# Head norms and merge sums in tiles of their own, the values' split apart from their transfer, sigmoids after the last exponentials, and the norm of x in pieces

## The chip, the cores and the metric

The kernel runs on one core of one Trainium2 chip. The metric is the device time of one execution in microseconds (us). Of the kernel before there are three timed runs and one profiled execution; all times below are of these.

## What is computed

One layer of a hybrid decoder trunk on 1024 positions of width 1024, in float32. Cut to what matters here:

```
h   = rms_norm(x, pre_mix_g)
qa, ka, va, qb, kb, vb, gates = split(h @ w_in)
# A: 4 heads, two maps of 64 columns each, values of 128
p   = softmax(causal(rope(qa) rope(ka)^T * scale))      # two maps for each head
oa  = (p[0] - lam * p[1]) @ va
oa  = rms_norm(oa, diff_head_g) * (1 - lam_init)        # the head norm
ya  = oa @ w_a_out
# B: 3 dilated groups (dilations 1, 4, 16), 4 heads of 128 each
o_g, lse_g = dilated_group(qb[g], kb[g], vb[g])         # softmax in a window
wts = softmax(stack(lse_g))                             # over the groups
yb  = sum(wts[g] * o_g) @ w_b_out                       # the merge
g_a, g_b = split(sigmoid(gates))
x   = x + rms_norm((g_a * ya + g_b * yb) @ w_mix_out, post_mix_g)
x   = x + rms_norm(conv_glu(rms_norm(x, pre_ffn_g)), post_ffn_g)
```

## The kernel before

A float32 operand is kept as two parts, a high one (`whi`, `xh`, `kh`, `vh`, `oah`), which ScalarE (ACT) copies out, and the low rest, which VectorE (DVE) subtracts (`split`, L149 and L146; `wlo`, `xl`, `kl`, ...). A product is then three matmuls on TensorE (PE): high by high, low by high, high by low (`mm3`, L154 to L156). `raw` is a weight as loaded.

The stages follow one another. **Values** (to about 160 us): the columns of V for all heads, by a scheme with seven products `p1` to `p7` for two halves `i` and four slices `k`, 56 steps `n`, that reads x unscaled. The evacuations go to `yv` (L471) and are stored to `v_d` by POOL's queue. Beside this run, at fixed steps, the angles, the norm of x (`norm_x`, sixteen squares, L389), the sines (L394), and `make_tables`: it spreads the norm's factor `rstd` over a row, transposes it on TensorE into a PSUM tile `acc`, and multiplies the tables of sine and cosine with it there (L406 to L408). `acc` is also what the products go to.

**Heads** (A, about 200 to 530 us): for each of four heads, eight blocks of queries. Scores (L717, L718) go to `s`, DVE adds the mask and takes the maximum (L720), ACT takes exponentials (L729), DVE joins both maps (L735), TensorE transposes them (L649, into `pt`), ACT and DVE split the transposed tile, and TensorE multiplies it with the values (`pv`, L662 and L665), into `o` and then `osb` (L759). After four blocks comes `head_norm`: the square `sq` of `osb` (L786), sums by products with ones (L794), a reciprocal root, the copy `spread` (L797), its transposes (L802). `sq` and `spread` come from the pool `rt` under the tags `t1` and `t2`, two buffers each, that the rotated projections (copies out of PSUM at L636, L637 to L639) and the gates (L249) also use. `jobs` yields after each block and runs what `later(n, fn)` has put on its clock of blocks; `interleave` puts pieces of the projections of the next head and of the gates, and values, between, as the letters of `A_FILLS` say.

**Groups** (B, about 530 to 915 us): twelve steps, one for a pair of heads, a group and a head, each with four blocks, the same way: mask and maximum (L921), exponentials (L928), the result `osb` to `og_d`. Values of a pair and group come back from `v_d` by `fetch_values` (SP's queue, tile `vperm`) and are split by ACT and DVE; `proj_b` makes q, then k of the next step (`kh`, L832). `merge(h)` joins the three groups of a head: from the sums' rows come weights, stored to `e_d`, loaded again broadcast as `mw` (L1019), beside the results `og` (L1021), both on POOL's queue; then `og` times `mw` in place (L1027), two sums into `og` itself (L1028, L1029), and a split or a store from there, for one half of the positions and then the other.

**Outputs** (from about 915 us): `branch` loads gates (`gl`), takes their sigmoid (L1092), and multiplies the merged results with the output weights; then the mix and the feed-forward part.

A tile framework orders the instructions of each engine: it simulates engine times, `high_priority` moves work ahead, and a tile with `bufs` buffers makes its next user wait for the readers of the last. Each engine then runs its list strictly in order.

Of the kernel before, what the change touches and what calls it, by code (L numbers as in the profile page):

```python
# [24 lines left out]
P = 128  # L25
# [24 lines left out]
START_GATES, A_FILLS, B_GATES = 1, ("gpgg", "gpvgg", "wgpgg", "gPVgg"), 3  # L50
SLOTS = 18
LEFT_PAD = 32


XT_BUFS, ANGLES_AT, NORM_AT, SINES_AT, TABLES_AT, STORE_AT = 6, 15, 18, 22, 29, {26: 0, 28: 3, 31: 2, 34: 1}
# [32 lines left out]
def trunk(ctx: ExitStack, tc: tile.TileContext, a, out):  # L88
# [119 lines left out]
    dma(gpre, a["pre_mix_g"])  # L208
# [174 lines left out]
    def norm_x():  # L383

        ssx = tiny.tile([P, 2, 32], F32, name="ssx", bufs=1)[:, :, :8]
        for m in range(8):
            for half, sl in enumerate(halves()):
                t = load_raw(a["x"][m * P : (m + 1) * P, sl], next(tags))
                nc.scalar.activation(t, t, AF.Square, accum_out=ssx[:, half, m : m + 1])  # L389
        tt(ssx[:, 0], ssx[:, 0], ssx[:, 1], ALU.add)  # L390
        nc.vector.tensor_copy(rstd, rsqrt(ssx[:, 0], D, tb, "rx"))
# [5 lines left out]
    def make_tables(*tab):  # L397
# [3 lines left out]
        for half, sl in enumerate(halves()):  # L401
            row = psum()
# [3 lines left out]
            nc.vector.scalar_tensor_tensor(neg[:, sl], tab[0][:, sl], -1.0, row, op0=ALU.mult, op1=ALU.mult)  # L406
            nc.vector.tensor_tensor(tab[0][:, sl], tab[0][:, sl], row, op=ALU.mult)
            nc.vector.tensor_tensor(tab[1][:, sl], tab[1][:, sl], row, op=ALU.mult)  # L408
# [18 lines left out]
    with ExitStack() as st_y:  # L427
# [12 lines left out]
        def fetch_v(n):  # L440
# [3 lines left out]
            got_v[n] = [load_raw(a["w_v"][j * 4 + k][:, (2 * i + c) * 512 : (2 * i + c + 1) * 512], next(tags), parts=1 if n else 2)  # L444
                        for c, j in which]

        def ready_v(n, w=512):
# [12 lines left out]
            for c in range(0, 512, w):  # L460
                split(*(t[:, c : c + w] for t in ready[n]), src[:, c : c + w])
# [67 lines left out]
        with ExitStack() as st0:  # L529
# [14 lines left out]
            for _ in range(4):  # L544
                nc.tensor.matmul(idle[:, :256], zeros[:, :P], zeros[:, :256], start=True, stop=True)
            for j in range(KC):
# [5 lines left out]
                for c in range(0, 512, w):  # L552
                    split_x(K_FIRST[j], slice(c, c + w), xts[j][:, c : c + w])
                    if c == 0:
                        ready_v(j, w)
# [18 lines left out]
        for n in range(8, len(steps_v)):  # L574
# [7 lines left out]
            if n == NORM_AT:  # L582
                norm_x()
# [115 lines left out]
    def attend_a(h, i, ops, vs, out_sb, pair):  # L699
# [52 lines left out]
        def add(b):  # L752
# [908 lines left out]
```

## Time and profile before

| | us |
|---|---|
| median of 3 runs (1754.65, 1761.11, 1761.55) | 1761.11 |
| profiled execution | 1758.33 |
| its span | 1756.6 |
| busy: PE / DVE / ACT / POOL | 1704.4 / 1345.0 / 893.7 / 100.6 |

The mean granted TensorE clock was 0.989 of full speed. The page cuts the span in 40 slices of 43.9 us and gives the busy share of each in tenths, 9 for 90% or more:

```profile
PE   9989998999989999989999999999999999999997
DVE  8884686777675676767656766699999999789977
ACT  7634564546343676546763633364444444355453
PEclk9999999999989999999999999999999999999999
DMA  8685311131212222532276442023222222196624
```

Slice 13 (about 483 to 527 us) has the clock at 0.8; the values fill the first four, the heads slices 6 to 12, the groups 13 to 21.

### The profile page before, as it was taken

Reading aid. Unit: us, or ns where it says so; the run is one execution under the profiler, and the core shown is the slowest. Engines: PE = TensorE matmul, PEld = TensorE weight load, DVE = VectorE, ACT = ScalarE, POOL = GpSimd, SP = SyncE. Lnnn points to the kernel's source line nnn. Section 1 sums busy time; section 2 is a strip of 40 time slices with the busy share of each in tenths; the row PEclk is TensorE's granted clock in tenths of the full one; section 3 lists DMA queues with packets and bytes.
Section 4 is the critical chain, followed back from the end, with each engine's and each line's share of the span. In section 5 each row is a group of like instructions: output and inputs, shape, how many; then the busy total and the mean of one; then the engine's idle time right before and its main releaser. Section 6 shows DMA issues by size and latency. Waiting matters only on the chain.

```text
span 1756.6 us, 23087 instructions
## 1 busy us (share of the span) xinstructions
PE 1704.4 (97%) x8076; PEld 1419.9 (81%) x8076; DVE 1345.0 (77%) x2558; ACT 893.7 (51%) x1648; POOL 100.6 (6%) x163
## 2 busy tenths in 40 slices
PE   9989998999989999989999999999999999999997
PEld 7778887788878888778878888878888888878886
DVE  8884686777675676767656766699999999789977
ACT  7634564546343676546763633364444444355453
POOL 0021000000000000200022410300000000000000
PEclk9999999999989999999999999999999999999999
DMA  8685311131212222532276442023222222196624
GB/s 254 195 303 183 111 61 39 40 102 59 80 61 77 74 73 74 176 114 73 82 257 233 160 156 96 36 73 108 90 78 97 78 78 96 55 336 217 215 84 156
DMA packets 105604, 216.42 MB, mean 123 GB/s; under 512 B 13120, under 2 KB 22272, under 8 KB 105488
## 3 DMA queue, kind: packets, MB, share of 16 engines
q1 hardware_dynamic: 91888, 176.79, 30.6%
q0 software_dynamic: 8704, 29.51, 5.0%
q10 hardware_dynamic: 4896, 8.65, 1.3%
q8 instruction: 63, 1.03, 0.2%
q14 instruction: 53, 0.43, 0.1%
HBM read 167.05 MB, written 47.86 MB: 122 GB/s over the span
## 4 chain that ended last, share of the span: by engine, by line
PE 49%; DVE 5%; DMA 4%; issue 2%; ACT 1%; POOL 0%; DVEq 0%; ACTq 0%; POOLq 0%; SPq 0%
PE acc L155 11%; PE acc L156 11%; PE acc L154 11%; PE acc L1497 3%; PE acc L1496 3%; PE acc L1495 3%; PE acc L1177 2%; PE acc L1179 2%; PE acc L1178 2%; PE pt L1495 1%; PE pt L1497 1%; PE pt L1496 1%; DMA og<-og_d 1%; DMA ot<-oa_d 1%; DVE t L1293 1%
## 5 line engine op out<-in xcount | busy, mean ns | idle before, releaser
L154 PE MATMUL acc<-xh,whi 128*128 128x512 f32 x768 | 306.8, 399 | 2.6 <-DVE gate L249 2.6
L155 PE MATMUL acc<-xh,wlo 128*128 128x512 f32 x768 | 306.4, 399 | 0.0
L156 PE MATMUL acc<-xl,whi 128*128 128x512 f32 x768 | 306.4, 399 | 0.0
L149 ACT ACTIVATE whi<-raw 128x512 fp32r<-128x512 f32 (+1 forms) x252 | 155.7, 626 | 218.9 <-PE acc L156 138.0
L146 DVE TENSOR_TENSOR wlo<-raw,whi 128x512 fp32r<-128x512 f32 (+1 forms) x252 | 177.2, 710 | 51.8 <-ACT whi L149 49.2
L154 PEld LDWEIGHTS acc<-xh,whi 128*128 128x128 f32 x768 | 146.4, 191 | 30.7 <-DVE gate L249 2.7
L155 PEld LDWEIGHTS acc<-xh,wlo 128*128 128x128 f32 x768 | 146.4, 191 | 28.2
L156 PEld LDWEIGHTS acc<-xl,whi 128*128 128x128 f32 x768 | 146.2, 190 | 28.0
L154 PE MATMUL acc<-mh,whi 128*128 128x512 f32 x400 | 155.8, 390 | 0.3 <-ACT mh L149 0.3
L155 PE MATMUL acc<-mh,wlo 128*128 128x512 f32 x400 | 155.6, 389 | 0.0
L156 PE MATMUL acc<-ml,whi 128*128 128x512 f32 x400 | 155.3, 389 | 0.0
L636 ACT ACTIVATE t<-acc 64x512 f32<-64x512 f32 (+1 forms) x160 | 94.7, 592 | 48.8 <-PE acc L156 42.7
L1373 DVE TENSOR_TENSOR u<-acc,u 128x512 f32<-128x512 f32 x133 | 90.6, 685 | 24.4 <-PE acc L156 24.3
L149 ACT ACTIVATE whi<-s 128x512 fp32r<-128x512 f32 x76 | 47.0, 628 | 108.3 <-PE acc L156 96.1
L637 DVE TENSOR_TENSOR t<-acc,cos 128x512 f32<-128x512 f32 x64 | 44.1, 689 | 58.5 <-ACT t L636 57.3
L154 PEld LDWEIGHTS acc<-mh,whi 128*128 128x128 f32 x400 | 75.1, 188 | 16.4 <-ACT mh L149 0.5
L155 PEld LDWEIGHTS acc<-mh,wlo 128*128 128x128 f32 x400 | 75.1, 188 | 15.6
L156 PEld LDWEIGHTS acc<-ml,whi 128*128 128x128 f32 x400 | 75.1, 188 | 15.6
L662 PE MATMUL o<-pt,vh 128*128 128x256 f32 (+1 forms) x376 | 72.3, 284 | 9.4 <-ACT pt L149 7.9
L1496 PE MATMUL acc<-whi,wlo 128*128 128x512 f32 x220 | 77.6, 390 | 0.0
L1495 PE MATMUL acc<-whi 128*128 128x512 f32 x220 | 76.5, 390 | 0.0
L662 PEld LDWEIGHTS o<-pt,vh 128*128 128x128 f32 x376 | 61.5, 197 | 16.0 <-ACT pt L149 8.9
(382 smaller groups left out, 3952.1 us busy)
## 6 DMA issues: line engine op xcount, KB each, us to landing
raw<-in_w_in SPq DMA_DIRECT2D x96, 256.0 KB, 2.9
raw<-in_w_up SPq DMA_DIRECT2D x88, 256.0 KB, 2.8
raw<-in_w_v SPq DMA_DIRECT2D x71, 256.0 KB, 4.0
raw<-c_d SPq DMA_DIRECT2D x48, 256.0 KB, 3.9
c_d<-c SPq DMA_DIRECT2D x22, 512.0 KB, 3.1
raw<-in_w_down SPq DMA_DIRECT2D x37, 256.0 KB, 3.6
v_d<-yv POOLq DMA_DIRECT2D x32, 256.0 KB, 5.3
gt_d<-gate ACTq DMA_DIRECT2D x32, 256.0 KB, 2.3
```

The costliest lines, as they stand in the source:

```text
L146: eng.tensor_tensor(lo, src, hi.bitcast(F32), op=ALU.subtract)
L149: nc.scalar.activation(hi, src, AF.Copy)
L154: nc.tensor.matmul(o, sh, mh, start=first, stop=False, skip_group_check=on)
L155: nc.tensor.matmul(o, sl, mh, start=False, stop=False, skip_group_check=on)
L156: nc.tensor.matmul(o, sh, ml, start=False, stop=last, skip_group_check=on)
L636: nc.scalar.activation(t1[dst], ps[src], AF.Copy)
L637: nc.vector.tensor_tensor(t2, ps, cos[:, sl], op=ALU.mult)
L662: nc.tensor.matmul(o[:, q0 : q1 + 1], vs[b // 4][0][:, b % 4, c], t[:, part], start=first and n == part == 0, stop=False)
L1373: nc.vector.tensor_tensor(to, made(p), x, op=ALU.add)
L1495: nc.tensor.matmul(banks[m], gh[:, tk], wh, start=f == 0, stop=False)
L1496: nc.tensor.matmul(banks[m], gl[:, tk], wh, start=False, stop=False)
L1497: nc.tensor.matmul(banks[m], gh[:, tk], wl, start=False, stop=f == NH - 1)
```

## The change

The number of steps and products is the same.

- **Head norms.** `sq` and `spread` get a tile `hn` with one buffer in the heads' own pool; `head_norm` is called at once when the fourth block is done, not three clock ticks later. The `rows` of `put_stats` also get a tile of their own.
- **Merge sums.** The product goes to `mw`, the sum of the last two to a new tile `om`; the small tiles go to a pool `merges`. The last sum comes at tick 9, not 8.
- **Values.** `fetch_values` is called before the step whose projection follows, the split between its q and its k. In the last head a letter `x` fetches and `V` splits.
- **Sigmoids.** Those of the first branch take a bias `zero`, made from the last sums of the exponentials. The four loads of `ot` share two tiles.
- **Norm of x** in eight pieces at steps 18 to 25; sines at 28, tables at 33, stores at 29, 30, 35 and 38. The transposed rows take a bank `s`, freed by an ACT copy alone; DVE multiplies with the copy `rstd_row`.
- **Start.** The load of `pre_mix_g` goes to POOL's queue, the first weight comes as one piece, and a small ACT copy stands ahead.

```diff
-START_GATES, A_FILLS, B_GATES = 1, ("gpgg", "gpvgg", "wgpgg", "gPVgg"), 3
+START_GATES, A_FILLS, B_GATES = 1, ("gpgg", "gpvgg", "wgpgg", "xgPVgg"), 3
...
-XT_BUFS, ANGLES_AT, NORM_AT, SINES_AT, TABLES_AT, STORE_AT = 6, 15, 18, 22, 29, {26: 0, 28: 3, 31: 2, 34: 1}
...
+XT_BUFS, ANGLES_AT, NORM_AT, SINES_AT, TABLES_AT, STORE_AT = 6, 15, 18, 28, 33, {29: 0, 30: 3, 35: 2, 38: 1}
...
-    dma(gpre, a["pre_mix_g"])
+    nc.gpsimd.dma_start(gpre, a["pre_mix_g"])
...
-    def norm_x():
-
-        ssx = tiny.tile([P, 2, 32], F32, name="ssx", bufs=1)[:, :, :8]
-        for m in range(8):
-            for half, sl in enumerate(halves()):
-                t = load_raw(a["x"][m * P : (m + 1) * P, sl], next(tags))
-                nc.scalar.activation(t, t, AF.Square, accum_out=ssx[:, half, m : m + 1])
-        tt(ssx[:, 0], ssx[:, 0], ssx[:, 1], ALU.add)
-        nc.vector.tensor_copy(rstd, rsqrt(ssx[:, 0], D, tb, "rx"))
+    ssx = tb.tile([P, 2, 8], F32, name="ssx")
+
+    def norm_x(m):
+
+        for half, sl in enumerate(halves()):
+            t = load_raw(a["x"][m * P : (m + 1) * P, sl], next(tags))
+            nc.scalar.activation(t, t, AF.Square, accum_out=ssx[:, half, m : m + 1])
+        if m == 7:
+            tt(ssx[:, 0], ssx[:, 0], ssx[:, 1], ALU.add)
+            nc.vector.tensor_copy(rstd, rsqrt(ssx[:, 0], D, tb, "rx"))
...
         for half, sl in enumerate(halves()):
-            row = psum()
+            row = psum(F32, ps_s, "s")
             for b in range(4):
                 nc.tensor.transpose(row[:, b * P : (b + 1) * P], spread[:, half * 4 + b], ident)
             nc.scalar.activation(rstd_row[:, sl], row, AF.Copy)
-            nc.vector.scalar_tensor_tensor(neg[:, sl], tab[0][:, sl], -1.0, row, op0=ALU.mult, op1=ALU.mult)
-            nc.vector.tensor_tensor(tab[0][:, sl], tab[0][:, sl], row, op=ALU.mult)
-            nc.vector.tensor_tensor(tab[1][:, sl], tab[1][:, sl], row, op=ALU.mult)
+        for sl in halves():
+            plus(neg[:, sl], tab[0][:, sl], -1.0, rstd_row[:, sl], ALU.mult)
+            tt(tab[0][:, sl], tab[0][:, sl], rstd_row[:, sl], ALU.mult)
+            tt(tab[1][:, sl], tab[1][:, sl], rstd_row[:, sl], ALU.mult)
...
-            for c in range(0, 512, w):
-                split(*(t[:, c : c + w] for t in ready[n]), src[:, c : c + w])
+            split(*ready[n], src)
...
+            nc.scalar.activation(rstd[:, 0:1], ones[:, 0:1], AF.Copy)
...
-            if n == NORM_AT:
-                norm_x()
+            if 0 <= n - NORM_AT < 8:
+                norm_x(n - NORM_AT)
+            if n == NORM_AT + 8:
                 lambda_scale()
...
                 if i % 4 == 1:
-
-                    if h + 1 < AH or i > 1:
-                        later(3, lambda: head_norm(h, i // 4, osb, eps4))
-                    else:
-                        head_norm(h, i // 4, osb, eps4)
+                    head_norm(h, i // 4, osb, eps4)
...
-        sq = rt.tile([P, 512], F32, tag="t1", name="sq")
+        sq = wk_a.tile([P, 512], F32, tag="hn", name="sq", bufs=1)
...
-            spread.append(rt.tile([P, 4, P], F32, tag="t2", name="spread"))
+            spread.append(wk_a.tile([P, 4, P], F32, tag="hn", name="spread", bufs=1))
...
-    def proj_b(g, h, res):
+    def proj_b(g, h, res, between=None):
...
         yield from proj_t(QB + g * 512 + h * P, put(qh, ql))
+        if between:
+            between()
         yield from proj_t(KB + g * 512 + h * P, put(kh, kl))
...
-    def values_of(pair, g):
-        return once(lambda: split_values(fetch_values(DIL[g], 512 + g * 512 + pair * 256), vs_b[pair, g])), 0
+    got_b = {}
+
+    def fetch_b(pair, g):
+        got_b[pair, g] = fetch_values(DIL[g], 512 + g * 512 + pair * 256)
+
+    def split_b(pair, g):
+        split_values(got_b.pop((pair, g)), vs_b[pair, g])
...
-                "V": lambda: values_of(0, 0),
+                "x": lambda: (once(lambda: fetch_b(0, 0)), 0),
+                "V": lambda: (once(lambda: split_b(0, 0)), 0),
...
-        rows = rt.tile([P, 512], F32, tag="t1", name="rows")[:n]
+        rows = wk_b[0].tile([P, 512], F32, tag="rows", name="rows", bufs=1)[:n]
...
         def add(half):
             sl = halves()[half]
             wt, og = got.pop(half)
-            nc.vector.tensor_tensor(og, og, wt, op=ALU.mult)
-            nc.vector.tensor_tensor(og[:, 0], og[:, 0], og[:, 1], op=ALU.add)
-            nc.vector.tensor_tensor(og[:, 0], og[:, 0], og[:, 2], op=ALU.add)
+
+            nc.vector.tensor_tensor(wt, og, wt, op=ALU.mult)
+            nc.vector.tensor_tensor(wt[:, 0], wt[:, 0], wt[:, 1], op=ALU.add)
+            o = wk_b[0].tile([P, 512], F32, tag="om", name="om", bufs=1)
+            nc.vector.tensor_tensor(o, wt[:, 0], wt[:, 2], op=ALU.add)
             if to is not None:
-                split(to[0][h][:, sl], to[1][h][:, sl], og[:, 0])
+                split(to[0][h][:, sl], to[1][h][:, sl], o)
             else:
-                dma(ob_d[h][:, sl], og[:, 0])
+                dma(ob_d[h][:, sl], o)
 
         def both():
             add(0)
             load(1)
 
-        return list(zip((0, 1, 2, 5, 8), (load_stats, weigh, lambda: load(0), both, lambda: add(1))))
-
-    def load_o(o, src, h, n=None):
-
-        t = slot("ot", dt=F32)
+        return load_stats, weigh, lambda: load(0), both, lambda: add(1)
+
+    def load_o(o, src, h, n, t=None):
+
+        t = t or slot("ot", dt=F32)
         dma(t, src[h])
-        if n is None:
-            return lambda: split(o[0][h], o[1][h], t)
         later(n, lambda: split(o[0][h], o[1][h], t))
...
-        todo = [functools.partial(attend_b, g, h, jj, ops_b[pair, g, h], vs_b[pair, g], sbs) for sbs in [[]] for jj in range(4)]
+        sbs = []
+        todo = [functools.partial(attend_b, g, h, jj, ops_b[pair, g, h], vs_b[pair, g], sbs) for jj in range(4)]
         nxt = steps[n + 1]
-        fills = [(proj_b(nxt[1], nxt[2], ops_b[nxt]), 8)]
         if h % 2:
-            fills.insert(0, values_of(*nxt[:2]))
-        interleave(jobs(todo), 4, *fills)
+            fetch_b(*nxt[:2])
+        interleave(jobs(todo), 4, (proj_b(nxt[1], nxt[2], ops_b[nxt], functools.partial(split_b, *nxt[:2]) if h % 2 else None), 8))
         if pair == 1 and g < 2 and h == 2:
-            for i, fn in merge(g):
+            for i, fn in zip((0, 1, 2, 5, 9), merge(g)):
                 later(i, fn, 0)
...
     pair, g, h = steps[-1]
+    ots = [slot("ot", dt=F32) for _ in range(2)]
     oa = [[slot(n) for _ in range(AH)] for n in ("oah", "oal")]
-    load_o(oa, oa_d, 0, 1)
-    load_o(oa, oa_d, 1, 1)
-    later(1, lambda: load_o(oa, oa_d, 2, 2))
-    later(2, lambda: load_o(oa, oa_d, 3, 2))
+    load_o(oa, oa_d, 0, 1, ots[0])
+    load_o(oa, oa_d, 1, 1, ots[1])
+    later(1, lambda: load_o(oa, oa_d, 2, 2, ots[0]))
+    later(1, lambda: load_o(oa, oa_d, 3, 2, ots[1]))
     ob = []
-    for i, fn in merge(2, ob):
-        later(i + 1, fn, 0)
-    todo = [functools.partial(attend_b, g, h, jj, ops_b[pair, g, h], vs_b[pair, g], sbs) for sbs in [[]] for jj in range(4)]
+    for i, fn in zip((1, 2, 3, 5, 9), merge(2, ob)):
+        later(i, fn, 0)
+    sbs = []
+    todo = [functools.partial(attend_b, g, h, jj, ops_b[pair, g, h], vs_b[pair, g], sbs) for jj in range(4)]
     interleave(jobs(todo), 4, gates(B_GATES))
+
+    zero = merges.tile([P, 1], F32, name="zero")
+    nc.vector.tensor_scalar(zero, sbs[1][:, 1, 7:8], 0.0, None, op0=ALU.mult)
...
-                nc.scalar.activation(gts[d], gts[d], AF.Sigmoid)
+                nc.scalar.activation(gts[d], gts[d], AF.Sigmoid, bias=zero)
```

The order of instructions moves as follows, at three places.

TensorE, in the middle of head 1 (the line numbers of the new file are 2 to 4 higher: its L652, L720, L721, L665 and L793 are L649, L717, L718, L662 and L794 of before). Before, from the sums of the square of head 0's last half:

```order
L794 MATMUL o<-ones,sq 128x1 x4
L649 MATMUL pt<-ident,s 128x128 x5
L717 MATMUL s<-k_2195,q_2193 128x256
L718 MATMUL s<-l_2197,q_2193 128x256
L662 MATMUL o<-pt,vh 128x256 x2
L665 MATMUL o<-pt,vl 128x256
L662 MATMUL o<-pt,vh 128x256 x2
L665 MATMUL o<-pt,vl 128x256
L662 MATMUL o<-pt,vh 128x256 x2
L662 MATMUL o<-pt,vh 128x128 x2
```

With the change, from the transposes to the first product with the values:

```order
L652 MATMUL pt<-ident,s 128x128 x6
L154 MATMUL acc<-xh,whi 128x512
L155 MATMUL acc<-xh,wlo 128x512
L156 MATMUL acc<-xl,whi 128x512
...
L154 MATMUL acc<-xh,whi 128x512
L155 MATMUL acc<-xh,wlo 128x512
L156 MATMUL acc<-xl,whi 128x512
L720 MATMUL s<-k_2192,q_2190 128x512
L721 MATMUL s<-l_2194,q_2190 128x512
L720 MATMUL s<-k_2192,q_2190 128x256
L665 MATMUL o<-pt,vh 128x256
L721 MATMUL s<-l_2194,q_2190 128x256
```

Between the transposes into `pt` and the first product with `vh` stood one pair of scores; now projection matmuls and scores stand there. The sums of the square stand some forty rows earlier.

VectorE and POOL at the merge of head 1. VectorE before, from the product of the second half on:

```order
L1027 TENSOR_TENSOR og<-og,mw 128x1536
L637 TENSOR_TENSOR t_7282<-acc,cos 128x512
L638 TENSOR_TENSOR t_7281<-t_7281,sin 128x512
L146 TENSOR_TENSOR wlo<-raw,whi 128x512
L1028 TENSOR_TENSOR og<-og 128x512
L921 ISA bs,bmx<-s,mask_b 128x128
L921 ISA bmx 128x1
L921 ISA bs,bmx<-s,mask_b 128x256
L921 ISA bmx 128x1
L639 TENSOR_TENSOR t_7282<-t_7282,t_7281 128x512
```

And with the change (L1036, L1037, L1039 are the product and the two sums; L640 to L642 the rotation; L832 the low half of k):

```order
L1036 TENSOR_TENSOR mw<-og,mw 128x1536
L642 TENSOR_TENSOR t_7283<-t_7283,t_7282 128x512
L929 ISA bs,bmx<-s,mask_b 128x128
L929 ISA bmx 128x1
L929 ISA bs,bmx<-s,mask_b 128x256
L929 ISA bmx 128x1
L1037 TENSOR_TENSOR mw<-mw 128x512
L933 TENSOR_SCALAR stat<-bmx 128x2
L832 TENSOR_TENSOR kl<-t_7283,kh 128x512
L1039 TENSOR_TENSOR om<-mw 128x512
```

The rotation's last step (L642) stands right behind the product, the values' splits (`vl`) are gone from between, and the last sum comes after the low half of k. POOL's queue of transfers at the same merge, before:

```order
L1021 DMA og<-og_d 128x3x512
L1013 DMA e_d<-me 128x3x8
L1021 DMA og<-og_d 128x3x512
L1019 DMA mw<-e_d 128x512 x6
L1021 DMA og<-og_d 128x3x512
```

With the change:

```order
L1027 DMA mw<-e_d 128x512 x3
L1021 DMA e_d<-me 128x3x8
L1027 DMA mw<-e_d 128x512 x3
L1029 DMA og<-og_d 128x3x512 x2
L1027 DMA mw<-e_d 128x512 x3
```

The second half's `og` now stands ahead of the second half's `mw`, right behind the first.

ScalarE at the end of the groups, before, from the last copies into `osb` and `kh` on:

```order
L955 ACTIVATE osb<-o 128x2x128
L832 ACTIVATE kh<-t_8549 128x8x64
L1092 ACT_TABLE_LOAD
L1092 ACTIVATE gl<-gl 128x1024
L250 DMA gt_d<-gate 128x512
L1092 ACTIVATE gl<-gl 128x1024
L149 ACTIVATE oah<-ot 128x1024
L955 ACTIVATE osb<-o 128x2x128
L140 ACTIVATE whi<-raw,ghead 128x512
L149 ACTIVATE oah<-ot 128x1024
L928 ACT_TABLE_LOAD
L928 ACTIVATE bs,stat<-bs,stat 128x128 x2
```

With the change:

```order
L831 ACTIVATE kh<-t_8555 128x8x64
L250 DMA gt_d<-gate 128x512
L963 ACTIVATE osb<-o 128x2x128
L149 ACTIVATE oah<-ot 128x1024
L140 ACTIVATE whi<-raw,ghead 128x512
L936 ACTIVATE bs,stat<-bs,stat 128x128 x2
L149 ACTIVATE oah<-ot 128x1024
L936 ACTIVATE bs,stat<-bs,stat 128x128 x2
L140 ACTIVATE whi<-raw,ghead 128x512
L250 DMA gt_d<-gate 128x512
L149 ACTIVATE pt<-pt 128x256
L936 ACTIVATE bs,stat<-bs,stat 128x128 x2
```

The table loads and the sigmoids (`gl`) have left this place, a copy of `ot` into `oah` stands between the two pairs of exponentials (L936) where both stood ahead of them, and the sigmoids come behind the last exponentials.

More of the change, by code (lines that the diff above doesn't have):

```diff
@@ L889, in trunk @@
                             pattern=[[-1, P]], channel_multiplier=1)
+    merges = open_pool(st_b, "merges", side="right")
     mask_2 = wk_b[0].tile([P, P], F32, name="mask_2")
@@ L992, in load_stats @@
         def load_stats():
-            r = got["r"] = tiny.tile([P, BG, 2, 8], F32, tag="mr", name="mr", bufs=2)
+            r = got["r"] = merges.tile([P, BG, 2, 8], F32, tag="mr", name="mr", bufs=2)
             side(r, st_d[h].rearrange("g a (p c) -> p g a c", c=8))
@@ L1005, in weigh @@
             nc.scalar.activation(e, e, AF.Exp)
-            f = tiny.tile([P, BG, 8], F32, tag="mf", name="mf", bufs=2)
+            f = merges.tile([P, BG, 8], F32, tag="mf", name="mf", bufs=2)
             nc.vector.tensor_tensor(f, e, den, op=ALU.mult)
@@ L1080, in trunk, with branch @@
     ob += [[mid_b.tile([P, S], F32R, tag=f"{n}{h}", name=n) for h in range(BH)] for n in ("obh", "obl")]
-    def branch(w_out, o, first, gate_tile, get_psum, scale=None):
+    def branch(w_out, o, first, gate_tile, get_psum, scale=None, zero=0.0):
         gts = []
@@ L1111, in gate_slot @@
         return tabs.tile([P, S], F32, tag=tag, name="gl") if tag else slot("gl", dt=F32)
-    for d, half, sl, ps, gt in branch(a["w_a_out"], oa, 0, gate_slot, psum, ghead):
+    for d, half, sl, ps, gt in branch(a["w_a_out"], oa, 0, gate_slot, psum, ghead, zero):
         nc.vector.tensor_tensor(ya[d][:, sl], ps, gt[:, sl], op=ALU.mult)
```

14 lines of the change are left out of this document (7 added, 7 removed).

## The prediction, written before the change was run

> **What bounds the kernel now.** I read the page first, then the waits of TensorE, then a table of windows cut at the stages, then the timelines around the longest stalls.
>
> ```profile
> span 1756.6 us, 23087 instructions
> PE 1704.4 (97%) x8076; PEld 1419.9 (81%) x8076; DVE 1345.0 (77%) x2558; ACT 893.7 (51%) x1648; POOL 100.6 (6%) x163
> ```
>
> TensorE is busy 97% of the span, so the change, which removes no product of the model, can win only in the 1756.6 − 1704.4 = 52.2 us in which TensorE stands idle, and in time that it spends at a lowered clock. The next view lists who ended TensorE's waits (us in total, times, longest).
>
> ```profile
> PE o L662 <- ACT pt L149: 7.9, 4, 2.8
> PE s L154 <- ACT kh L832: 6.8, 2, 6.0
> PE pt L649 <- ACT bs L928: 5.5, 4, 2.8
> PE acc L154 <- DVE cos L408: 3.5, 1, 3.5
> PE acc L154 <- ACT yv L471: 2.8, 2, 2.4
> PE acc L154 <- DVE gate L249: 2.6, 1, 2.6
> PE s L154 <- ACT whi L149: 1.9, 1, 1.9
> ```
>
> No bandwidth is missing here: these are small waits for an evacuation or a vector result that came late in its engine's order. The windows (length, then busy us of PE, PEld, DVE, ACT and POOL, granted clock, DMA share, GB/s) place them:
>
> ```profile
> 60.00:130.00 70.00, 62.76 (x275) 50.28 (x274) 57.99 (x111) 36.30 (x76) 12.16 (x20) 1.00 0.83 274
> 280.00:530.00 250.00, 232.92 (x1195) 197.63 (x1194) 181.35 (x528) 129.44 (x264) 0.00 (x0) 0.95 0.20 64
> 690.00:800.00 110.00, 99.56 (x523) 82.60 (x522) 75.32 (x178) 60.11 (x132) 11.98 (x19) 0.97 0.40 127
> 880.00:930.00 50.00, 47.16 (x234) 39.41 (x234) 27.57 (x66) 31.82 (x54) 10.65 (x18) 0.97 0.73 254
> 930.00:1756.00 826.00, 815.16 (x3618) 672.94 (x3617) 697.94 (x1029) 365.16 (x601) 54.65 (x80) 1.00 0.38 128
> ```
>
> Length minus PE busy is the idle time: 7.2 us in the values stage, 17.1 in the attention of the heads, 10.4 in the groups (the merges), 2.8 at their end, 37.5 in all. The 10.8 us after 930 stay: from the gates of branch B on, every engine's order is the same in both kernels. Four of the five rows also show what the stalls leave behind, a granted clock under 1.00. Narrow windows price it:
>
> ```profile
> 300.00:315.00 15.00, 10.53 (x41) 8.32 (x42) 12.18 (x42) 9.46 (x19) 0.00 (x0) 0.77 0.13 43
> 345.00:355.00 10.00, 7.21 (x32) 6.38 (x33) 9.12 (x32) 7.33 (x19) 0.00 (x0) 0.83 0.13 37
> 430.00:435.00 5.00, 4.60 (x21) 4.26 (x22) 4.94 (x21) 2.56 (x10) 0.00 (x0) 0.66 0.39 105
> 500.00:520.00 20.00, 14.98 (x74) 13.10 (x75) 17.43 (x60) 11.40 (x28) 0.00 (x0) 0.74 0.17 53
> 765.00:780.00 15.00, 9.03 (x41) 7.32 (x40) 13.09 (x26) 9.01 (x19) 0.00 (x0) 0.77 0.28 91
> 900.00:905.00 5.00, 4.87 (x16) 3.69 (x17) 2.66 (x10) 3.26 (x14) 0.41 (x1) 0.66 0.89 283
> ```
>
> Busy time times (1 − clock) is what the slow clock cost: 10.53·0.23 + 7.21·0.17 + 4.60·0.34 + 14.98·0.26 = 9.1 us in the heads, 2.1 in the merges, 1.7 at the end. Within reach lie 37.5 + 12.9 = 50.4 us, and up to 1.9 at the start.
>
> **Head norms (the largest term).** Squares and spreads get a tile of their own instead of sharing two buffers with the rotated keys and the gates.
>
> ```profile
> 343.69 0.74 PE L649 MATMUL pt<-ident,s 128*128 128x128 f32 x5
> 343.87 2.39 ACT L636 ACTIVATE t<-acc 32x512 f32<-32x512 f32 x4 [1.14 <-PE o L794]
> 346.80 0.60 ACT L149 ACTIVATE pt<-pt 128x512 fp32r<-128x512 f32 x1
> 347.45 0.38 PE L662 MATMUL o<-pt,vh 128*128 128x256 f32 x1 [2.78 <-ACT pt L149]
> 305.17 0.42 DVE L797 COPY spread<-rhy 128x512 f32<-128x512 f32 x1
> 305.50 0.68 DVE L249 TENSOR_TENSOR gate<-acc,rstd_row 128x512 f32<-128x512 f32 x1
> ```
>
> (Here and below, rows of several engines' timelines stand together: start, length, engine, what it does, and in brackets its idle time before and what ended it.) ACT's four copies of a projection (2.39 us) waited 1.14 us for the sums that read the square in their buffer; behind them, in order, stood the copy of the transposed weights, and behind that TensorE, for 2.78 us. At 305 the gate followed the spread and TensorE's projection waited 2.6 us for it (the row of the waits above). In the order of the change, transposes and the products that need them stand further apart: there five transposes and one pair of scores, then the first product; now six transposes, eighteen projection matmuls and more. At the spacing of the stage (25 us hold 112 such matmuls, so 0.22 us each) that is 4 us of cover against a stall of 2.78. Over the stage my count of what lies between gives under 1.6 us at each of the twelve stall places before, and nowhere under 3.9 after. The instructions stay, eight squares, sums and spreads. The new tile has one buffer, so a square waits for the transposes of the spread before it, but that is a half head, 250/8 = 31 us, earlier. What the cover does not reach is unknown: from nothing won to all 17.1 + 9.1 = 26.2. I take 23.5, one stall of 2.7 left, nearest to the row at 347.45.
>
> *Clock.* The rows say that a dip follows stalls also where none is long (0.83 after 2.78 us at 347), while the 3.46 us before `L154` in the values stage left 1.00. The Trainium skill, TensorE: Matmul & The Clock Gate, section "What's actually happening", has the clock halved after an idle window of some 3.4 us. The trace agrees only in part, since the stalls at 305 and 347 are shorter; by that page alone the heads' dips would not be the stalls' doing, which is the first rival.
>
> **Values stage.** The norm of x goes in eight pieces, the tables come later and through a bank that one ACT copy frees.
>
> ```profile
> L389 ACT ACTIVATE raw<-raw 128x512 f32<-128x512 f32 x16 | 9.9, 627 | 5.0 <-DMA raw<-in_x 5.0
> 117.27 0.68 DVE L408 TENSOR_TENSOR cos<-cos,acc 128x512 f32<-128x512 f32 x1
> 114.08 0.88 DVE L498 TENSOR_SCALAR yv<-yv,edge 128x512 f32<-128x512 f32 x2
> ```
>
> Sixteen squares, 9.9 us on ACT, stood close together in front of evacuations: 2.8 us of TensorE's wait. `L408` held the accumulator until 117.95: 3.5. The short waits beside them make up 7.2. After the change nothing reads the rows' bank but ACT. What comes instead is a run of twelve of the scalings of 0.44 us on DVE in front of a weight split, 5.3 us where four to eight stood; it may cost 0 to 2. The DMA share of 0.83 leaves a fetch that comes late as the other risk. Bounds 0 to 7.2; I take 5.2.
>
> **Merges and values of the groups.**
>
> ```profile
> 750.02 1.76 DVE L1027 TENSOR_TENSOR og<-og,mw 128x1536 f32<-128x1536 f32 x1 [4.64 <-DMA mw<-e_d]
> 752.54 0.69 DVE L1029 TENSOR_TENSOR og<-og 128x512 f32<-128x512 f32 x1
> 758.24 0.76 POOL L1021 DMA_DIRECT2D og<-og_d  x1 [4.55 <-DMA ob_d<-og]
> 765.37 1.06 ACT L149 ACTIVATE vh<-vperm 128x1024 fp32r<-128x1024 f32 x1 [7.39 <-DMA vperm<-v_d]
> 765.71 1.76 DVE L1027 TENSOR_TENSOR og<-og,mw 128x1536 f32<-128x1536 f32 x1 [8.75 <-DMA og<-og_d]
> 771.07 0.63 ACT L832 ACTIVATE kh<-t 128x512 fp32r<-128x512 f32 x1 [3.19 <-DVE t L639]
> 740.12 1.68 POOL L1019 DMA_DIRECT2D mw<-e_d  x3
> ```
>
> The second half of `og` could be fetched only when the sum had been stored from the same tile: the sum ended at 753.23, the fetch left at 758.24, and DVE stood 8.75 us in order, with the rotation of the keys behind it, 6.0 us of TensorE. Now the products go to `mw` and the sum to `om`, so `og` is free at 751.8 and only `mw` waits, for the last sum. From issue to use `mw` took 750.02 − 740.12 = 9.9, so the second product starts near 753.2 + 9.9 = 763.1 at the latest, 2.6 earlier; from there to the keys' high half stand one product, one rotation and one copy, 1.76 + 0.68 + 0.63 = 3.1, against 771.70 − 765.71 = 6.0. Together 5.5 of the 6.0. The values' fetch leaves half a step sooner ((880 − 530)/12/2 = 15 us), so ACT's 7.39 goes, which else would be late next. The other 4.4 us of the stage wait for `mw`, whose fetch is not shorter: I take 0.3 of them. With 1.9 of the clock's 2.1 that is 7.7; bounds −4.6 (`mw` late again at the first half, as at 750.02) to 12.5.
>
> **End of the groups.** Sigmoids wait for a zero made from the last sums, so two table loads go.
>
> ```profile
> 887.03 1.28 ACT L1092 ACT_TABLE_LOAD   x1
> 897.22 1.06 ACT L149 ACTIVATE oah<-ot 128x1024 fp32r<-128x1024 f32 x1 [2.08 <-DMA ot<-oa_d]
> 898.29 1.28 ACT L928 ACT_TABLE_LOAD   x1
> 899.59 0.40 ACT L928 ACTIVATE bs<-bs,stat 128x128 f32<-128x128 f32 x1
> ```
>
> The load at 898.29 stood just ahead of the exponentials for which TensorE waited 2.8 us. But the copy of `ot` at 897.22 waited for a transfer, and the change keeps one such copy between the two pairs of exponentials, now reusing tiles. Bounds 0 to 2.8 + 1.7; I take 2.2, half. The rows show the exponential 0.02 us behind the load. The Trainium skill, ScalarE: Activation LUTs, section "What ACT_TABLE_LOAD costs", adds a drain of 1.38 us to a load of 1.28; no gap of that size stands here, and with it the sum would come to 1.4 us more gain.
>
> **Start.** The gains' load goes to POOL's queue, the first weight comes in one piece, a copy brings a 1.28 us table load forward. TensorE waited 1.9 us there for a split weight. ACT issues a transfer behind that load, so −1.3 to +1.9 won; I take 0.5.
>
> **Sum.** 23.5 + 5.2 + 7.7 + 2.2 + 0.5 = 39.1 us, less 2 for new short waits: 37. The profiled execution took 1758.33 us, 1.7 over its span and 2.8 under the median of 1761.11 (1754.65 to 1761.55). 1758.3 − 37 = **1721 us**.
>
> **Rivals.**
> - *The dips stay.* If the clock falls for the mix of short products in the heads and not for the stalls, 9.1 + 1.9 + 0.8 of clock is not won: 1733 us. For it: the skill's rule above. Against: the stage's rows without stalls show 1.00, and every dip starts at one. Chance 0.07.
> - *New waits in the old places.* Twelve DVE scalings, `mw` behind the sum, two `ot` tiles: V gives 2, the heads half of 26.2, the groups 3, the end nothing: 18, so 1740 us. For it: DVE is in order, and 77% busy. Against: the distances in the order. Chance 0.19.
> - *Nothing happens.* The squares stand ahead of the copies in ACT's order also now; if ACT's order and not the tile held TensorE, and the others as well give back what they win, it is 1755 ± 5. Against: 2.39 us of copies began when the sums ended. Chance 0.05.
> - *Slower.* The fetch of the values waits on the slots that TensorE frees, and SP's queue is in order, with the projection's weights behind it. If these slots come free only at the middle of the step, the weights behind are up to 15 us late, less the lead that they have (one weight unit is 48 matmuls of 0.22 us, up to 10). From 37/6 = 6 us for each of six fetches the change loses; at 8, with 1.7 of clock as at 900, it is 6·9.7 − 37 = +21, 1779 us. Against: TensorE's idle time has no weight's transfer in it now. Chance 0.03.
>
> **How the numbers follow.** The forecast has 0.66, with its own bounds 1710 to 1732. Reaching to the first rival and half of the second gives 1708 to 1742, over 0.8. Half a per cent, about what a measurement of this kernel can tell from no change, is 8.8 us: faster takes the forecast, the dips and nearly all of the new waits, 0.91; same 0.06; slower 0.03.
>
> **What would show it.** PE idle in the heads' stage under 5 us and the clock at 1.00 from 280 to 530; no wait of TensorE for `cos`, `gate` or `kh` over 1 us; the second `og` fetch issued within 1 us of the first product; no table load ahead of the last exponentials. It is wrong if TensorE waits for `pt` or `vh` over 2 us as often as now, if the clock in the heads stays at 0.95 without stalls, or if a weight's transfer appears among TensorE's waits.

## The result, and the profile after

| | median us (runs) | lowest to highest | profiled execution, span |
|---|---|---|---|
| before | 1758.38 (4) | 1754.65 to 1761.55 | 1758.33, 1756.6 |
| changed | 1728.82 (4) | 1727.60 to 1731.44 | 1729.41, 1727.5 |

The ratio is 0.9835, 95% interval 0.9807 to 0.9862: 29.6 us faster where 37 were forecast, inside the range. The page of the changed kernel:

```profile
span 1727.5 us, 23075 instructions
PE 1693.0 (98%) x8076; PEld 1414.2 (82%) x8076; DVE 1344.2 (78%) x2558; ACT 889.2 (51%) x1646; POOL 100.8 (6%) x164
```

TensorE's idle time fell from 52.2 to 34.5 us, and its busy time by 11.4 for the same 8076 matmuls: fewer of them ran at a lowered clock (it cost 12.9 us before, and 2.5 + 1.6 us in the same stages now). The waits of TensorE, changed kernel (us in total, times, longest):

```profile
PE acc L154 <- ACT yv L470: 6.8, 1, 6.8
PE s L154 <- ACT kh L831: 3.6, 2, 2.6
PE s L154 <- ACT xh L362: 3.3, 1, 3.3
PE pt L652 <- ACT bs L936: 2.1, 2, 1.1
PE s L154 <- DVE bmx L929: 1.9, 1, 1.9
PE acc L154 <- DVE ya L1127: 1.4, 1, 1.4
```

`pt`, `gate`, `cos` and the `kh` of 6 us have left the head of the list. A wait of 6.8 us for `yv` is new. The stage windows of the changed kernel (columns as in the prediction):

```profile
60.00:130.00 70.00, 67.92 (x299) 54.85 (x298) 55.96 (x107) 36.07 (x75) 10.67 (x17) 1.00 0.78 257
130.00:280.00 150.00, 143.21 (x650) 118.97 (x650) 93.38 (x183) 77.23 (x132) 8.94 (x17) 0.98 0.37 122
280.00:530.00 250.00, 250.00 (x1338) 214.54 (x1337) 193.87 (x560) 134.96 (x272) 0.00 (x0) 1.00 0.22 71
530.00:690.00 160.00, 159.90 (x892) 137.68 (x891) 112.46 (x281) 109.21 (x239) 5.58 (x11) 1.00 0.26 85
690.00:800.00 110.00, 104.26 (x562) 88.37 (x562) 77.26 (x170) 62.97 (x136) 8.46 (x14) 0.98 0.39 122
800.00:880.00 80.00, 77.89 (x418) 65.84 (x417) 54.55 (x133) 51.21 (x107) 6.37 (x10) 1.00 0.39 133
880.00:930.00 50.00, 48.58 (x222) 40.12 (x221) 26.77 (x53) 23.05 (x32) 12.81 (x23) 1.00 0.77 257
```

From 280 to 530 us TensorE is never idle and never slowed: 1338 matmuls where 1195 stood. In the values stage the idle time is 2.1 + 6.8 us where it was 7.2, so nothing was won there. The new wait, in the changed kernel's timelines (start, length, engine):

```profile
129.25 2.18 SPq L126 DMA_DIRECT2D raw<-in_xT  x2
...
138.27 0.72 ACT L362 ACTIVATE xh<-raw,edge 128x512 fp32r<-128x512 f32 x1 [3.65 <-DMA raw<-in_xT]
140.50 0.63 ACT L149 ACTIVATE whi<-raw 128x512 fp32r<-128x512 f32 x1 [1.50 <-DVE raw L320]
141.03 0.67 ACT L470 ACTIVATE yv<-acc,edge 128x512 f32<-128x512 f32 x1
...
141.75 0.79 PE L154 MATMUL acc<-whi,t3h 128*128 128x512 f32 x1 [6.79 <-ACT yv L470]
```

Read from the bottom: TensorE needs a bank that ACT must evacuate; ACT, in order, stood first behind the last of four late pieces of x, whose fetch had left only after 129 us. In a window of its own the stall also shows its slow clock, 0.14 of 18.2 busy us, 2.5 us more:

```profile
125.00:150.00 25.00, 18.21 (x70) 14.25 (x69) 16.42 (x28) 9.04 (x15) 2.16 (x4) 0.86 0.69 228
```

### The profile page after: what moved, and what is told of

It is laid out like the page before. It is cut to its first block, busy times and chain, and to the rows that moved or that the text cites. A ratio compares the mean times of both kernels' runs of the same rounds, so it can differ in the third digit from the quotient of the medians.

```text
span 1727.5 us, 23075 instructions
## 1 busy us (share of the span) xinstructions
PE 1693.0 (98%) x8076; PEld 1414.2 (82%) x8076; DVE 1344.2 (78%) x2558; ACT 889.2 (51%) x1646; POOL 100.8 (6%) x164
## 5 line engine op out<-in xcount | busy, mean ns | idle before, releaser
L149 ACT ACTIVATE whi<-raw 128x512 fp32r<-128x512 f32 x251 | 155.9, 628 | 198.3 <-PE acc L156 121.3
L146 DVE TENSOR_TENSOR wlo<-raw,whi 128x512 fp32r<-128x512 f32 x251 | 179.3, 722 | 42.5 <-ACT whi L149 41.6
L640 DVE TENSOR_TENSOR t<-acc,cos 128x512 f32<-128x512 f32 x64 | 44.1, 690 | 51.4 <-ACT t L639 50.4
L1510 PE MATMUL acc<-wlo,whi 128*128 128x512 f32 x220 | 73.3, 390 | 0.0
L723 DVE CUSTOM_DVE_ANT_0 s<-s,mask_a 128x512 f32<-128x512 f32 (+3 forms) x96 | 51.7, 553 | 25.4 <-PE s L721 16.8
```

The lines of the kernel that those rows point to most:

```text
L146: eng.tensor_tensor(lo, src, hi.bitcast(F32), op=ALU.subtract)
L149: nc.scalar.activation(hi, src, AF.Copy)
L640: nc.vector.tensor_tensor(t2, ps, cos[:, sl], op=ALU.mult)
L723: nc.vector.tensor_tensor_reduce(out=s_sb[:, c0:c1], in0=ps, in1=mask, scale=1.0, scalar=-3.0e38, op0=ALU.add, op1=ALU.max, accum_out=mx[: ...
L1510: nc.tensor.matmul(banks[m], gh[:, tk], wl, start=False, stop=f == NH - 1)
```

## The experiments

Twelve kernels, each timed with runs of the kernel before on the same chip, whose medians lay between 1758.27 and 1759.01. Medians are compared with the 1728.82 of the change (1727.60 to 1731.44). In the diffs, `...` stands for lines left out.

**1. The head norms as before, in the changed kernel.**

```diff
-        sq = wk_a.tile([P, 512], F32, tag="hn", name="sq", bufs=1)
+        sq = rt.tile([P, 512], F32, tag="t1", name="sq")
...
-            spread.append(wk_a.tile([P, 4, P], F32, tag="hn", name="spread", bufs=1))
+            spread.append(rt.tile([P, 4, P], F32, tag="t2", name="spread"))
...
-                    head_norm(h, i // 4, osb, eps4)
+                    if h + 1 < AH or i > 1:
+                        later(3, lambda: head_norm(h, i // 4, osb, eps4))
+                    else:
+                        head_norm(h, i // 4, osb, eps4)
```

> The changed kernel with the head norms as before: square and spread in the shared two buffers of the rotated keys and the gates, called three ticks late. Theory (the norms are what freed the heads' stage): TensorE idle again some 17 us between 280 and 530 us, clock near 0.95 there, and the time some 26 us up, 1750 to 1758. Rival (the order was shuffled anyway, the norms are one of several edits that gave it): under 10 us up, below 1740.

1749.15 us (1747.56 to 1752.32), ratio 0.9950 (0.9935 to 0.9966): 20.3 us up, a little under the theory's range. The stage windows of this kernel for the heads and the merges:

```profile
280.00:530.00 250.00, 236.51 (x1213) 200.10 (x1212) 181.74 (x530) 128.62 (x264) 1.17 (x4) 0.95 0.20 63
530.00:690.00 160.00, 160.00 (x873) 137.08 (x872) 103.83 (x252) 96.51 (x205) 0.88 (x1) 1.00 0.23 78
690.00:800.00 110.00, 109.46 (x598) 93.18 (x597) 85.41 (x204) 67.78 (x150) 11.96 (x19) 1.00 0.41 133
```

The stalls and the slow clock are back in the heads, 13.5 us idle and 0.05 of 236.5 (11.8): 25. That the time rose by 20 only shows behind them, where both kernels have the changed form: this one has 4.4 us of idle time from 530 to 930 us (0.5 in the last row), the change 9.4. Part of what the heads win is given back there.

**2. and 3. Which half of it: the tile or the call.** Number 2 puts both tiles back into `rt` and keeps the direct call (the first four lines of the diff above), number 3 keeps the tile and calls late (the last five).

> The changed kernel with square and spread in the shared buffers, but still called at once. If the shared tile holds ACT and DVE: idle time of TensorE in the heads 10 to 20 us, 1745 to 1757. If the late call was the cause: at most 3 us of idle time there, 1726 to 1733.

> The changed kernel with the tile of their own, but called three ticks late as before. If the shared tile was the cause: 1726 to 1733, TensorE idle under 3 us in the heads. If the late call was it: 10 to 20 us idle there, 1745 to 1757.

With the shared tile 1749.21 us (1748.54 to 1750.89), with the late call 1727.74 (1725.54 to 1729.41). The heads' window, first of the shared tile:

```profile
280.00:530.00 250.00, 241.78 (x1229) 204.27 (x1228) 184.17 (x518) 127.07 (x253) 1.14 (x4) 0.96 0.22 70
```

and of the own tile, called late:

```profile
280.00:530.00 250.00, 250.00 (x1332) 214.06 (x1330) 188.58 (x546) 133.50 (x271) 0.00 (x0) 1.00 0.23 73
```

With the shared tile the stretch ahead, 130 to 280 us, has 5.3 us more idle time than the change's, so it is 13.5 in all, as in number 1. The tile is the cause; when the norm is called makes no difference that these runs can tell. The framework makes the engines' orders anew with each tile, so whether the buffers that come free or the order that follows from them does it is not separated.

**4. The gains' load back on SP's queue.**

```diff
-    nc.gpsimd.dma_start(gpre, a["pre_mix_g"])
+    dma(gpre, a["pre_mix_g"])
```

> The changed kernel with the load of the gains back on SP's queue, first in it. If the gains' late landing sets the start: the first real matmul at 6.5 to 7.0 us instead of 8.3, the time 1.3 to 2 us down (1727). If the first weight or the table load sets it: first matmul at 8.0 or later, no change. The rest of the kernel is in the same order, so nothing else moves.

1727.75 us (1727.43 to 1728.40). The changed kernel's first activation of x and first product:

```profile
7.73 0.51 ACT L362 ACTIVATE xh<-xt,edge 128x256 fp32r<-128x256 f32 x1 [1.70 <-DMA edge<-in_pre_mix_g]
...
8.29 1.22 PE L154 MATMUL s<-whi,xh 128*128 128x512 f32 x2 [3.26 <-ACT xh L362]
```

and the first product with the load on SP:

```profile
6.51 0.50 PE L154 MATMUL s<-whi,xh 128*128 128x512 f32 x1 [1.49 <-ACT whi L149]
```

The first product comes 1.8 us sooner, and the first 60 us hold 1.3 us less idle time and 238 products instead of 226: here they follow each other after 0.23 us from the start, in the change after 0.43 until 13.1 us. The medians differ by 1.1, with ranges that overlap; the wait itself is settled by the rows.

**5. The table work of the values stage later.**

```diff
-XT_BUFS, ANGLES_AT, NORM_AT, SINES_AT, TABLES_AT, STORE_AT = 6, 15, 18, 28, 33, {29: 0, 30: 3, 35: 2, 38: 1}
+XT_BUFS, ANGLES_AT, NORM_AT, SINES_AT, TABLES_AT, STORE_AT = 6, 15, 18, 34, 40, {36: 0, 38: 3, 41: 2, 44: 1}
```

> The changed kernel with the sines, the transposed rows, the six table products and the stores of the scaled values at later steps (tables at 40), so that DVE has no table product ahead of the low halves of x of the last columns. Theory (these products delay the freeing of the raw buffers, so the fetch of x comes late and ACT stands in order behind it): the wait for yv of 6.8 us falls under 2, the clock stays at 1.00 from 125 to 150, and the time falls by 6 to 9, 1720 to 1723. Rival (the fetch of x is late because the transfers are full there, whatever DVE does): the wait stays at 5 or more and the time within 2.

1729.52 us (1729.13 to 1733.14). A miss for both: the wait for `yv` fell to 3.6, but not under 2, and the time did not fall. The idle time from 60 to 280 us went from 8.9 to 6.5, and TensorE's clock in that profile was 0.98 from 60 to 130 us, against 1.00. DVE's table products explain at most part of the wait.

**6. The stores of the tables on POOL's queue**, so that SP's queue does not stand behind the last product. The order of TensorE, DVE and ACT is that of the change.

```diff
-            dma(to, t)
+            nc.gpsimd.dma_start(to, t)
```

> The changed kernel with the three stores of the tables on POOL's queue instead of SP's; the order of TensorE, DVE and ACT stays. If SP's queue, standing behind the store that waits for the last table product, holds the fetches of weights and x: they go 2 to 3 us sooner and the wait for yv at 140 falls from 5 to 7 to 2 to 4 us, time 2 to 4 down, 1725 to 1727. If the raw buffers or full transfers hold them: unchanged within 1.

1728.64 us (1727.90 to 1729.60). The last two fetches of x left at 128.68 instead of 129.25, the wait was 6.2. The stores' place in SP's queue is not what holds them.

**7. The norm of x in one piece**, at step 18 as before; sines, tables and stores stay at the steps of the change.

```diff
...
-            if 0 <= n - NORM_AT < 8:
-                norm_x(n - NORM_AT)
-            if n == NORM_AT + 8:
+            if n == NORM_AT:
+                norm_x()
```

(The lines left out put the sixteen squares into one loop again.)

> The changed kernel with the norm of x in one piece at step 18. If the pieces took ACT's squares away from the evacuations: the waits for yv near 60 to 80 us of 2.8 us in all come back, the wait of 5 to 7 us at 140 stays, 1731 to 1734. If the squares stood out of the way anyway: within 1 of 1728.8.

1724.06 us (1722.37 to 1725.98), ratio 0.9805 (0.9782 to 0.9829): the fastest of all, 4.8 under the change, on the side that neither case had. Its timelines:

```profile
123.70 3.38 SPq L126 DMA_DIRECT2D raw<-in_xT  x2
...
133.36 0.72 ACT L362 ACTIVATE xh<-raw,edge 128x512 fp32r<-128x512 f32 x1 [3.62 <-DMA raw<-in_xT]
...
79.28 0.50 PE L154 MATMUL acc<-whi,t4h 128*128 128x512 f32 x1 [0.88 <-ACT yv L473]
```

In one piece, the squares cost TensorE 0.9 us at 79, not 2.8 (the kernel before waited 2.4 there: with ACT in the same order, TensorE now came 0.8 us later and ACT's copy ended 0.7 sooner). The last fetches of x leave 5.5 us sooner, and the wait at 140 is 3.8. So the pieces, meant to free ACT, made the stage slower: from 60 to 280 us it has 5.2 us of idle time and 1.5 of slow clock here, 8.9 and 2.5 in the change.

The queue's rows show the way. All loads of weights and of x go through the same `raw` buffers in turn, from SP's queue in order, and a square frees its buffer only when it has run. The sixteen loads for the squares leave from 58.77 to 84.37 us in the change and from 58.90 to 76.93 here, the weights behind them from 85.89 and 78.16 on, and the first of the four late pieces of x, in the change and here, at:

```profile
113.42 0.33 SPq L126 DMA_DIRECT2D raw<-in_xT  x1
...
104.97 1.42 SPq L126 DMA_DIRECT2D raw<-in_xT  x1
```

**8. The merges' sums in `og` again.**

```diff
-            nc.vector.tensor_tensor(wt, og, wt, op=ALU.mult)
-            nc.vector.tensor_tensor(wt[:, 0], wt[:, 0], wt[:, 1], op=ALU.add)
-            o = wk_b[0].tile([P, 512], F32, tag="om", name="om", bufs=1)
-            nc.vector.tensor_tensor(o, wt[:, 0], wt[:, 2], op=ALU.add)
+            nc.vector.tensor_tensor(og, og, wt, op=ALU.mult)
+            nc.vector.tensor_tensor(og[:, 0], og[:, 0], og[:, 1], op=ALU.add)
+            nc.vector.tensor_tensor(og[:, 0], og[:, 0], og[:, 2], op=ALU.add)
+            o = og[:, 0]
...
-            for i, fn in zip((0, 1, 2, 5, 9), merge(g)):
+            for i, fn in zip((0, 1, 2, 5, 8), merge(g)):
...
-    for i, fn in zip((1, 2, 3, 5, 9), merge(2, ob)):
+    for i, fn in zip((1, 2, 3, 6, 9), merge(2, ob)):
```

> The changed kernel with the products and sums of a merge in og again, as before, and the last sum at the tick of before. Theory (og held until the sum is stored delays the second half): one or two waits of DVE for og of 7 us or more, TensorE's waits for kh 5 us or more in all beyond the 3.6 of the change, time 4 to 8 up, 1733 to 1737. Rival (what counts is only where DVE stands when a load lands): within 3 of 1729, either way.

1731.54 us (1728.56 to 1731.66): the sign of the theory, under its size and inside the rival's 3, and the ranges overlap. The mechanism is there in the timelines of this kernel:

```profile
726.80 0.76 POOL L1029 DMA_DIRECT2D og<-og_d  x1 [5.25 <-DMA ob_d<-og]
...
734.63 1.76 DVE L1036 TENSOR_TENSOR og<-og,mw 128x1536 f32<-128x1536 f32 x1 [7.77 <-DMA og<-og_d]
...
740.66 0.58 PE L154 MATMUL s<-kh,qh 128*128 128x256 f32 x1 [5.25 <-ACT kh L831]
```

In the change the same place reads:

```profile
727.94 1.63 POOL L1027 DMA_DIRECT2D mw<-e_d  x3 [2.81 <-DVE om L1039]
...
738.06 1.76 DVE L1036 TENSOR_TENSOR mw<-og,mw 128x1536 f32<-128x1536 f32 x1 [5.52 <-DMA mw<-e_d]
...
741.13 0.39 PE L154 MATMUL s<-kh,qh 128*128 128x256 f32 x1 [2.56 <-ACT kh L831]
```

The wait has changed its name from `og` to `mw`: DVE waits 22.2 us for both in this kernel's products, 25.7 in the change's, but the rest of the rotation follows sooner (3.1 us from the product to TensorE's next row, against 6.0), so TensorE waits 2.6 and not 5.3.

**9. The groups' values fetched and split at one place.**

```diff
+        fills = [(proj_b(nxt[1], nxt[2], ops_b[nxt]), 8)]
         if h % 2:
-            fetch_b(*nxt[:2])
-        interleave(jobs(todo), 4, (proj_b(nxt[1], nxt[2], ops_b[nxt], functools.partial(split_b, *nxt[:2]) if h % 2 else None), 8))
+            fills.insert(0, (once(lambda: (fetch_b(*nxt[:2]), split_b(*nxt[:2]))), 0))
+        interleave(jobs(todo), 4, *fills)
```

> The changed kernel with the groups' values fetched and split at one place again, at the start of the step's fills (only the first fetch, in the last head, stays early). Theory (ACT stands behind the fetch, in order): ACT waits some 7 us for vperm at one or two steps, TensorE 3 to 6 us behind it, 1732 to 1737. Rival (ACT's wait was off the path, og's was the one that counted): within 2 of 1729.

1730.39 us (1728.72 to 1730.55). ACT again waits for `vperm`, 5.3 us in three places, against 0.4 in the change; TensorE's waits shift from `kh` to `bmx` and `kl`, 5.0 us in these two against 2.1. The time lies in the rival's range, and its runs overlap with those of the change.

**10. The first branch's sigmoids without the zero.**

```diff
-    for d, half, sl, ps, gt in branch(a["w_a_out"], oa, 0, gate_slot, psum, ghead, zero):
+    for d, half, sl, ps, gt in branch(a["w_a_out"], oa, 0, gate_slot, psum, ghead):
```

> The changed kernel with the first branch's sigmoids free of the zero, so that two table loads come back ahead of or between the last exponentials; the order of the other engines stays. Theory: 1.3 to 4 us up, 1730 to 1733, and a wait of TensorE for bs of 2 to 3 us more. Rival (the copies of ot, not the loads, set that place): within 1.

1730.18 us (1727.52 to 1730.57), and the waits for `bs` 1.9 us against 2.1. The median is at the edge of the theory's range, but the runs overlap with those of the change, and two more table loads cost TensorE nothing at that place that the profile shows.

**11. and 12. The kernel before with the own tile alone.** To make room, the sums of the norm of x and the merges' small tiles move to other pools, as in the change. Number 12 is the same with one more line:

```diff
-LEFT_PAD = 32
+LEFT_PAD = 48
```

> The kernel before with one thing of the change: square and spread in a tile of their own, still called three ticks late (the sums of the norm of x and the small tiles of the merges move to other pools to make room). Theory (the tile alone carries the gain, the other edits together are worth little): 1730 to 1738, no idle time of TensorE from 280 to 530. Rival (the edits are worth what they were costed at, the merges 8, the values 5): 1740 to 1748.

> The kernel before with the own tile for square and spread, as in b_norm_tile, and the padding of the left pools at 48 instead of 32, as in the change; the order of TensorE is that of b_norm_tile. In b_norm_tile 100 us of the feed-forward part hold 438 matmuls where before and the change hold 442 or 443, at a clock of 1.00. If where the tiles lie sets that (the moved small tiles are 1088 bytes, 64 over a multiple of 128; the padding adds the 64): 443 matmuls again, the time from the first product of the mix to the end 745 to 747 us instead of 750.4, and 5 to 10 us down, 1732 to 1737. If that profile's rate was something of that execution: 1741 again with 442 or 443.

1741.52 us (1740.78 to 1744.88), and with the padding 1737.63 (1736.61 to 1739.40), ratio 0.9880 (0.9862 to 0.9897). One window of the feed-forward part, without the padding:

```profile
1200.00:1300.00 100.00, 100.00 (x438) 82.14 (x437) 93.76 (x126) 44.15 (x59) 1.19 (x12) 1.00 0.25 87
```

and with it:

```profile
1200.00:1300.00 100.00, 100.00 (x443) 82.84 (x442) 94.11 (x127) 43.05 (x58) 1.20 (x12) 1.00 0.28 92
```

The padding moves only addresses, and TensorE's order is the same, row by row. Number 6, timed beside number 11 on the same chip, holds 443 in this window too. So 3.9 us, less than the 5 to 10 expected, are a matter of where tiles lie. Number 11 fell into the rival's range; with the addresses put right, number 12 is at the edge of the theory's, and the tile, with the room made for it, wins 21.2 us of the 29.6. In that kernel the heads have no idle time, but the groups and their end have 14.6 from 530 to 930 us where before had 13.3 and the change has 9.4. The other edits together are worth 8.8 us. None of the merges, the groups' values and the sigmoids showed more than 2.7 by itself, and the pieces of the norm lose 4.8 (7), so what carries the 8.8 is not shown.

## Why the prediction came out as it did

- **Head norms: right in mechanism, and nearly in size.** Forecast 23.5 with one stall left, the stage shows 17.1 + 9.1 = 26.2 gone. The tile causes it (1 to 3). The call, which the prediction did not cost, does nothing.
- **The clock, first rival: it fell.** No idle time, no dip: 1.00 through the heads in every kernel with the own tile, 0.95 or 0.96 in those without. By the Trainium skill's rule of some 3.4 us of idle time (TensorE: Matmul & The Clock Gate, section "What's actually happening") the heads' dips, behind stalls of at most 2.8, should not have been theirs and should have stayed; the measurement decides.
- **Values stage: the step that failed.** Forecast +5.2 in a range from 0, measured 7.2 before against 8.9 of idle time and 2.5 of clock after, −4.2. The steps "2.8 for the squares" and "3.5 for the bank" were read rightly as waits, and both are gone. The error was to take the wait behind the squares for the price of having them in one piece, and to give the eight pieces no price: with the squares in one piece (7) the stage costs 6.7, so the pieces lose 4.7 and the other edits of the stage win 0.5. What came instead was named as a risk, "a fetch that comes late", but not priced: the last fetch of x, 6.8 us. The run of twelve scalings, which had a price, has no wait beside it but one of 0.5 and one of 1.4 us.
- **Merges and values: mis-sized.** Forecast 7.7; 10.4 + 2.1 before stand against 0.1 + 5.7 idle and 1.6 of clock (0.07 of the 23.0 busy us between 700 and 725), 5.1 won. The transfer took 10.1 us from issue to use, 9.9 were taken, and the 3.1 us from product to keys were 3.07. But the residue of 0.5 came from a TensorE that reaches the keys as late as before, 12.5 us behind the sum; it came 11.0 behind it, the fetch left 0.4 behind it, and the wait was 2.6. So the sign "no wait for `kh` over 1 us" did not come; those for `cos`, `gate`, the second `og` (issued at 724.37, its buffer's reader done at 723.92) and the table load did.
- **End of the groups: mis-sized.** Forecast 2.2, measured 2.8 + 1.7 against 2.1 + 1.4: 1.0. The table loads were not the price, as far as number 10 shows.
- **Start: wrong sign.** Forecast +0.5 in a range from −1.3, measured −1.4 (first product at 8.29, 6.91 before). The step counted the load ahead on ACT and gave the move to POOL's queue no cost; that queue was 1.3 of the 1.4 (4). With the products that ran slowly there the loss is a little larger, 226 products by 60 us where before had 234.
- **Sum.** 26.2 − 4.2 + 5.1 + 1.0 − 1.4 = 26.7, of 29.1 between the profiles; 2.4 are not placed, and a dip of the clock at 1150 us in the changed kernel alone, 1.7 us, goes the other way. The forecast's 39.1 less 2 differ from it mainly by the values (9.4). Values and start left their own bounds; that the total stayed inside its range is the heads' doing, and in part luck, since they gave 2.7 more than was taken. The second rival, new waits in the old places, was right for the values and wrong for the heads, and gave 1740.
- **Two slips of reading.** Three of the five window rows, not four, show a clock under 1.00 (0.95, 0.97, 0.97), and the slice with the clock at 0.8 is the twelfth. Neither enters the sum.

## What to carry to other kernels

A scratch tile that shares its buffers with a busier stage's tiles ties that stage to the scratch's slowest reader: a small tile of its own was worth more than every reordering here. A wait's length is no price of what ended it; ask what is second, and give every late fetch that is named as a risk a term. And when tiles move between pools, compare a stage that nothing touched: its matmuls per window show whether an address has moved, too.

## What the runs showed of the hardware that was not expected

- **Addresses.** Moving 1088 bytes of small tiles took the dense matmuls of the feed-forward part from 443 to 438 for 100 us at a granted clock of 1.00; 64 bytes of padding brought it back (12). Which tile it is was not tried.
- **A load of gains on POOL's queue.** Issued from 1.29 to 1.97 us, it was first used at 7.73; from SP's queue x could use it at 3.13, when the wait was for x itself (4).
- **The clock.** A wait of 1.87 us at 705.5 stands in a window of 0.93, waits of 1.02 and 2.56 in the next 25 us leave 1.00; the 3.46 us at 118 in the kernel before left 1.00, and 3.05 at the same place in number 11 brought a dip. So the length of one stall does not decide it. The traces' record of the clock shows what more there is: up to the last matmul every slow stretch that they hold is at half clock, lasts 3.41 us, twice or three times that, and begins on a grid of that step, one grid for each trace. The 3.46 us fall on two cells of it, idle to 0.53 and 0.49, the 3.05 us mostly on one, idle to 0.84; the 2.78 us at 347 on one, idle to 0.78, the 1.87 us on one, idle to 0.58, and these three have a slow cell behind them. So the same wait can cost a dip or not, as it falls on the grid. The idle share from which the clock drops was not worked out, and cells near a half go either way. The first 60 us show 0.97 in some profiles and 1.00 in others, but that is no difference of the start: in the change (1.00) the first products stand 0.43 us apart until 13.1 us, in number 7 (0.97) until 12.0, then 0.23; the change's record of the clock begins only at 13.3.
